# A row sum of squared differences: its 4 KB result stored by two queues instead of one

## The chip, the cores and the metric

The kernel runs on one core of a Trainium2 chip. The metric is the device time of one execution in microseconds, given as the median of several executions. The profile is taken from one more execution and lists what each engine and each DMA queue did and when. In it DVE is VectorE, ACT is ScalarE, POOL is GpSimd, SP is SyncE, and SPq is SP's own sequencer, which issues DMAs and waits for semaphores. PE, the matrix engine, has no work here.

## The reference

```
def setup_inputs():
    batch, dim = 1024, 4096
    return {
        "x": np.random.randn(batch, dim).astype(np.float32),
        "y": np.random.randn(batch, dim).astype(np.float32),
        "axis": -1,
    }

def reference(x, y, axis):
    return np.sum((x - y) ** 2, axis=axis).astype(np.float32)
```

Two float32 matrices of 16 MiB each are read, and 1024 float32 numbers, 4 KB, are written.

## The kernel before

Eight rows lie on each of the 128 partitions: partition p holds rows 8p to 8p+7, one after the other, as 32768 numbers. A transfer of some columns is thus one stretch per partition. The result has the same layout: `results` is a tile of 128 partitions by 8 numbers, and partition p's eight numbers, 32 B, go to one stretch of the output.

`X` and `Y` in the core's memory hold six of the eight rows each. Rows 6 and 7 go into the places of rows 0 and 1 once those have been squared. The loads are cut into the widths `xw` and `yw`: large ones first, small ones towards the end, so that little work is left when the last one has landed. All loads are issued by SP (`load`, L108), two of them ahead of the start-up barrier; those that go into used places wait for ACT (L221). Each load has a semaphore of its own.

DVE goes through the loads of `Y` in the order in which they are issued. For each it waits for the data, then subtracts in place (`sub`, L176) in pieces that don't cross a row. ACT squares each piece with an activation that sums along the row (`square`, L182); its sums go into `parts`, or into `results` where a row has one piece alone. DVE adds the parts of a row together (`complete`, L189). The last piece, 128 columns of row 3, is squared on DVE itself (L205) and adds the other part of its row; after it DVE completes row 7, the last sum of all. The order on each engine is the order of the program text: no scheduler moves anything. The engines are held together by the semaphores `diffs` (DVE to ACT), `acts` (ACT to DVE and SP) and `sums` (the sums that DVE has finished).

The end is this:

```
    nc.sync.wait_ge(sums, n["sums"])
    nc.sync.dma_start(out=ov, in_=results).then_inc(stored, 16)
    prog.close(nc.sync, stored, 16)
```

SP waits until all sums are there, issues one store of the whole of `results` (L233), and then goes into `close`. That clears the semaphores of the program in one range (L44) and waits until the store's completions have brought `stored` to 16 (L45), taking them away again. A DMA brings its semaphore up by 16 when all of it has landed. `stored` itself is not in the range that is cleared. Every semaphore made by `prog.semaphore` is, so that the next execution finds them at zero.

Of the kernel before, what the change touches and what calls it, by code (L numbers as in the profile page):

```python
# [47 lines left out]
def kernel(tc, x, y, axis, out):  # L48
    nc = tc.nc
    P = nc.NUM_PARTITIONS  # L50
# [11 lines left out]
    ov = out.rearrange("(p r) -> p r", p=P)  # L62
# [5 lines left out]
    results = nc.alloc_sbuf_tensor("results", [P, R], F32).ap()  # L68
# [22 lines left out]
    prog = Program(nc, tc)  # L91
    stored = nc.alloc_semaphore("stored")
    diffs = prog.semaphore("diffs")
    acts = prog.semaphore("acts")
    sums = prog.semaphore("sums")
    n = dict(diffs=0, acts=0, sums=0)

    def home(c0, c1):
        h0 = c0 % H
        return slice(h0, h0 + c1 - c0)  # L100
# [86 lines left out]
    def complete(r):  # L187
        nc.vector.wait_ge(acts, squared[row_parts[r][-1]])
        nc.vector.tensor_reduce(  # L189
            out=results[:, r : r + 1],  # L190
            in_=parts_of(r, len(row_parts[r])),
            axis=mybir.AxisListType.X,
            op=add,
        ).then_inc(sums, 1)
        n["sums"] += 1

    for j, (c0, c1) in enumerate(ys):
        final = j == len(ys) - 1
        wait_loaded(c1, landed_y[j][1])
        for piece in pieces_of(j, c0, c1):  # L200
            sub(*piece)
            r = piece[0] // D
            if final:
                nc.vector.wait_ge(diffs, n["diffs"])
                nc.vector.tensor_tensor_reduce(  # L205
                    out=Y[:, home(*piece)],
# [22 lines left out]
                complete(r)  # L229
    complete(7)  # L230

    nc.sync.wait_ge(sums, n["sums"])
    nc.sync.dma_start(out=ov, in_=results).then_inc(stored, 16)  # L233
    prog.close(nc.sync, stored, 16)


# [33 lines left out]
```

## Time and profile before

| what | value |
|---|---|
| median of 13 runs | 84.05 us (83.95 to 84.17) |
| the profiled execution's own time | 83.99 us |
| its span, first to last instruction | 82.7 us |
| DVE busy | 36.8 us (45%) |
| ACT busy | 33.4 us (40%) |
| DMA packets, bytes | 2736, 33.56 MB, mean 406 GB/s |
| share of 16 DMA engines in use | 95.9% |
| start of the store's issue on SP | 81.21 us |

The profiled execution took 83.99 us, of which the span accounts for 82.7; the rest lies before the first and behind the last instruction. All packets went over one hardware queue, SP's. Times inside the profile are counted from the start of the span. Waits and DMA issues of a sequencer are not counted as busy; the landing time of a DMA is counted from the start of its issue. The chain of waits is followed back from the last instruction that does work, at each step to what released it.

### The profile page before, as it was taken

The numbers are of one execution on the slowest core, as the hardware profiler recorded it, in microseconds if no ns is written. First come the engines' busy times: TensorE is split into PE (matmuls) and PEld (weight loads), VectorE is DVE, ScalarE is ACT, GpSimd is POOL, SyncE is SP. The second block draws the span as 40 slices with busy tenths as digits, with TensorE's granted clock in tenths as the row PEclk, the third lists the DMA queues.
The fourth block names the chain that finished last, engine by engine and source line by source line (L and its number), as shares of the span: only waits on it lengthen the run. The fifth ranks groups of instructions, "written<-read, shape, count | busy, mean of one in ns | idle before, by whom it ended". The sixth has DMA issues, their size and how long they took to land.

```text
span 82.7 us, 136 instructions
## 1 busy us (share of the span) xinstructions
DVE 36.8 (45%) x27; ACT 33.4 (40%) x41; POOL 0.2 (0%) x4
## 2 busy tenths in 40 slices
DVE  0000000000000000000299999999189996989982
ACT  0500000000000000000000979889896999899991
POOL 0000000000000000000000000000000000000000
DMA  6998998888999992899599899969989799999960
GB/s 135 396 484 381 618 523 381 381 381 381 504 503 503 503 503 126 378 503 503 254 507 507 349 412 507 476 285 507 413 350 508 344 442 440 420 407 410 398 213 2
DMA packets 2736, 33.56 MB, mean 406 GB/s; under 512 B 432, under 2 KB 1328, under 8 KB 1712
## 3 DMA queue, kind: packets, MB, share of 16 engines
q1 hardware_dynamic: 2736, 33.56, 95.9%
HBM read 33.55 MB, written 0.00 MB: 406 GB/s over the span
## 4 chain that ended last, share of the span: by engine, by line
DMA 63%; SPq 16%; DVE 12%; ACT 4%; issue 1%
DMA Y<-in_y_dram 63%; SPq L108 16%; DVE X L176 11%; ACT X L182 4%; DVE Y L205 0%; DVE results L189 0%; SPq L221 0%; DVE results L205 0%
## 5 line engine op out<-in xcount | busy, mean ns | idle before, releaser
L176 DVE TENSOR_TENSOR X<-X,Y 128x2048 f32<-128x2048 f32 (+10 forms) x21 | 36.2, 1779 | 44.4 <-DMA Y<-in_y_dram 44.1
L182 ACT ACTIVATE X<-X 128x2048 f32<-128x2048 f32 (+9 forms) x20 | 31.2, 1560 | 45.6 <-DVE X L176 45.6
L182 ACT ACTIVATION_READ_ACCUMULATOR X<-X 128x1 f32 x20 | 3.7, 186 | 0.0
L182 ACT ACT_TABLE_LOAD x1 | 1.3, 1283 | 1.9 <-PEq L19 1.9
L189 DVE TENSOR_REDUCE results<-parts 128x1 f32<-128x2 f32 (+2 forms) x4 | 0.4, 148 | 0.0
L205 DVE CUSTOM_DVE_ANT_0 Y<-X,parts 128x128 f32<-128x128 f32 x1 | 0.4, 351 | 0.0
L251 POOL MEMSET const-bfloat16-1.0<- 128x1 bf16 x1 | 0.1, 101 | 0.0
L251 POOL MEMSET const-uint8-127<- 128x1 uint8 x1 | 0.1, 101 | 0.0
L251 POOL MEMSET const-float32-0.0<- 128x1 f32 x1 | 0.1, 98 | 0.2 <-issue 0.2
L251 POOL MEMSET const-float32-1.0<- 128x1 f32 x1 | 0.1, 98 | 0.0
L205 DVE DVE_READ_ACCUMULATOR2_ANT results<- 128x1 f32 x1 | 0.1, 83 | 0.0
## 6 DMA issues: line engine op xcount, KB each, us to landing
Y<-in_y_dram SPq DMA_DIRECT2D x1, 8128.0 KB, 39.0
X<-in_x_dram SPq DMA_DIRECT2D x1, 6144.0 KB, 21.3
X<-in_x_dram SPq DMA_DIRECT2D x1, 4096.0 KB, 48.3
Y<-in_y_dram SPq DMA_DIRECT2D x1, 4096.0 KB, 57.5
X<-in_x_dram SPq DMA_DIRECT2D x1, 2736.0 KB, 13.3
X<-in_x_dram SPq DMA_DIRECT2D x1, 2048.0 KB, 7.2
Y<-in_y_dram SPq DMA_DIRECT2D x1, 1392.0 KB, 18.9
Y<-in_y_dram SPq DMA_DIRECT2D x1, 1312.0 KB, 16.1
```

The source lines that it names most:

```text
L108: nc.sync.dma_start(out=dst[:, home(c0, c1)], in_=src[:, c0:c1]).then_inc(sem, 16)
L176: nc.vector.tensor_sub(out=a, in0=a, in1=Y[:, home(c0, c1)]).then_inc(diffs, 1)
L182: nc.scalar.activation(out=a, in_=a, func=Square, accum_out=acc).then_inc(acts, 1)
L189: nc.vector.tensor_reduce(out=results[:, r : r + 1], in_=parts_of(r, len(row_parts[r])), axis=mybir.AxisListType.X, op=add,).then_inc(sums, 1)
L205: nc.vector.tensor_tensor_reduce(out=Y[:, home(*piece)], in0=X[:, home(*piece)], in1=X[:, home(*piece)], scale=1.0, scalar=parts_of(r, 1), ...
L251: nc = _bacc.Bacc("TRN2", target_bir_lowering=False, num_devices=1)
```

## The change

The store is cut into two halves by partitions. ACT waits for all sums and issues the store of the upper 64 partitions on its own queue; SP waits for the same and issues the store of the lower 64. Both count up `stored`, which now has to reach 32. Since `close` clears `sums` among others, SP must not begin it while ACT may still be waiting for `sums`; so ACT counts up a new semaphore `begun` behind its DMA, and SP waits for that before `close`.

```diff
@@ -93,6 +93,7 @@
     diffs = prog.semaphore("diffs")
     acts = prog.semaphore("acts")
     sums = prog.semaphore("sums")
+    begun = prog.semaphore("begun")
     n = dict(diffs=0, acts=0, sums=0)
@@ -229,9 +230,15 @@
                 complete(r)
     complete(7)
 
+
+    half = P // 2
+    nc.scalar.wait_ge(sums, n["sums"])
+    nc.scalar.dma_start(out=ov[half:P], in_=results[half:P]).then_inc(stored, 16)
+    nc.scalar.sem_inc(begun, 1)
     nc.sync.wait_ge(sums, n["sums"])
-    nc.sync.dma_start(out=ov, in_=results).then_inc(stored, 16)
-    prog.close(nc.sync, stored, 16)
+    nc.sync.dma_start(out=ov[0:half], in_=results[0:half]).then_inc(stored, 16)
+    nc.sync.wait_ge(begun, 1)
+    prog.close(nc.sync, stored, 32)
```

## The prediction, made before the changed kernel had run

> **What bounds the kernel now.** I read the timeline of the last microseconds first, because the diff touches only what follows the last sum; then SP's waits, the DMA view of the store alone, and last the chain of waits over the whole span.
>
> The end of the timeline (start, duration, engine, line, operation):
>
> ```profile
> 80.54 0.36 ACT L182 ACTIVATE X<-X 128x192 f32<-128x192 f32 x1
> 80.73 0.35 DVE L205 CUSTOM_DVE_ANT_0 Y<-X,parts 128x128 f32<-128x128 f32 x1
> 80.80 0.19 ACT L182 ACTIVATION_READ_ACCUMULATOR X<-X 128x1 f32 x1
> 81.01 0.08 DVE L205 DVE_READ_ACCUMULATOR2_ANT results<- 128x1 f32 x1
> 81.02 0.16 DVE L189 TENSOR_REDUCE results<-parts 128x1 f32<-128x8 f32 x1
> 81.21 0.34 SPq L233 DMA_DIRECT2D out_dram<-results  x1
> ```
>
> ACT is finished at 80.99 (80.80 + 0.19). The last sum ends at 81.18 (81.02 + 0.16), and SP begins the store 0.03 us later. From 81.21 to the end of the span at 82.7 nothing computes: this tail of about 1.45 us is the store alone, and all that the change can act on.
>
> SP's queue, waits from 78 us on (who waited for whom, total us, times, longest):
>
> ```profile
> SPq L233 <- DVE results L189: 8.1, 1, 8.1
> SPq L45 <- SPq L45: 1.0, 1, 1.0
> ```
>
> L45 is the last wait, in `close`, for the store's 16 completions. It stands open for 1.0 us: between issue and landing SP has only the range clear of the semaphores to do (L44, 68 ns, at 81.6).
>
> The DMA view from 82.0 to 82.5 (40 slices of 12.5 ns), and the store's line from the window 80 to 83:
>
> ```profile
> DMA  0000146853446343210000000000000000000000
> GB/s 0 0 0 3 13 28 41 44 24 19 26 28 29 23 19 16 11 5 5 0 0 0 0 0 0 0 0 0 0 0 0 0 0 0 0 0 0 0 0 0
> DMA packets 144, 0.00 MB, mean 8 GB/s; under 512 B 144, under 2 KB 144, under 8 KB 144
> ```
>
> ```profile
> out_dram<-results SPq DMA_DIRECT2D x1, 4.0 KB, 1.4
> ```
>
> The store is 128 rows of 32 B: 128 data packets and 16 completions, 144 in all, nine on each of 16 engines. They run from 82.04 to 82.23 (the first and the last slice that move anything). In the window 80 to 83 they take 2.6% of 16 engines' 3 us, so 0.026 x 3 x 16 / 144 = 8.7 ns each; one engine works 9 x 8.7 = 0.08 us. So the tail divides into four: **issue** 0.34 (81.21 to 81.55), **way to the engines** 0.49 (to 82.04), **packets** 0.19 (to 82.23), **receipt** about 0.4 (to 82.6, 1.4 us after the start of the issue). The engines are in use for 0.19 us of 1.4 and never more than eight tenths busy: the tail is latency, not bandwidth.
>
> The chain of waits, over the whole span, says that the rest is out of reach:
>
> ```profile
> DMA 63%; SPq 16%; DVE 12%; ACT 4%; issue 1%
> DMA Y<-in_y_dram 63%; SPq L108 16%; DVE X L176 11%; ACT X L182 4%; DVE Y L205 0%; DVE results L189 0%; SPq L221 0%; DVE results L205 0%
> ```
>
> The loads bind, and they are all issued before the first edited line. The chain ends at L189; the store's flight behind it appears in no share.
>
> **What the Trainium skill says.** "DMA: Bandwidth & Descriptors", section Rules for kernel authors, says of two transfers to disjoint partition halves not to bother: each half spreads over all 16 engines, from either queue, so they share them. The trace has one queue only, but agrees on the spread (144 packets, 16 completions). The section Anatomy of one DMA puts most of a small DMA's fixed time into the write receipt and the completion; here receipt and way, 0.4 and 0.49, are most of the 1.4. "Perfetto Trace Analysis", section DMA Instruction — HWDGE, says that an issue first waits for a lock on a descriptor generator which the issuing sequencers share, and that the recorded issue includes that wait. In this trace only SP issues, so two issues at once are not shown.
>
> **The change part by part.** The profiled execution took 83.99 us with its span of 82.7, so 1.29 lie around it; it is 0.06 below the median of 84.05. I work out what the tail gains or loses and add that to both.
>
> 1. *Everything before 81.18.* The instruction lists of the two kernels are the same on DVE and POOL, on SP up to the store, and on ACT up to a DMA row behind its last Activation. The loads, their waits and the order are untouched: 0. ACT's new wait for `sums` has no instruction of ACT queued behind it but the new DMA and the increment of `begun`, and nobody else waits for ACT's sequencer then. ACT's last row ends at 80.99, 0.19 before the sums are there, so ACT stands at its wait in time: 0.
>
> 2. *ACT picks up `sums`.* SP needed 0.03 (81.18 to 81.21). ACT's pauses behind DVE in the chain are 0.02 to 0.03. Both start at about 81.21: 0. Low end 0, high end 0.1 if a queue that has issued no DMA wakes more slowly.
>
> 3. *SP's half.* SP issues 64 rows instead of 128. Its issues last 0.33 to 0.34 after a wait (the load at 53.49, the store) and mostly 0.43 to 0.49 back to back, whether for 2624 or for 960 columns: the size of a row does not show. The number of rows is 128 in all of them, so half of it is not shown: between 0.17 (all scales) and 0.34 (none). I take 0.34, because the price did not follow the amount otherwise: 0.
>
> 4. *ACT's half.* One DMA issue on a queue that shows none before. Low end 0.17, as above; high end 0.68, if the generator is locked for the whole of SP's issue (0.34 + 0.34). I take 0.44, the usual price of an issue that follows directly on another: part of it behind SP's, most of it beside it. That is 0.10 after SP's: **+0.10**. It lies on the path, since the end waits for 32 completions and the later half sets them.
>
> 5. *Way, packets, receipt.* The way (0.49) and the receipt (0.4) begin anew for each half, side by side: 0. Data packets stay 128; completions go from 16 to 32, so each engine has 10 packets instead of nine: **+0.01**. Should each half's packets come out in half the time, up to 0.09 (half of 0.19) comes back; I take none of it, since both halves meet on the same engines.
>
> 6. *The wait for `begun`, the increment, one semaphore more in the clear.* Queued behind it on SP are the clear (68 ns) and the last wait. `begun` comes when ACT's issue ends, in my sum at 81.21 + 0.44 = 81.65, plus some 0.03; before, the clear stood at 81.6. The work that hides this is the store's own flight, the 1.0 us of L45. With that cover gone it would cost 0.1; to use it up, ACT's issue would have to end after 82.5, and then its half would land late anyway. 0.
>
> 7. *Around the span.* A second hardware queue may have to be made ready or put away, which no trace here shows. If the 1.29 around the span hold a share per queue, it is a fraction of them: low end 0, high end 0.3 as an estimate. I take 0.
>
> Sum: +0.10 + 0.01 = +0.11. On the profiled execution that is 84.10; on the median 84.05 + 0.11 = **84.16 us**. Changes of 0.2% (0.17 us) are about what a measurement of this kernel can tell from no change, and this lies within.
>
> **The rivals.**
> - *A, side by side (the forecast):* the later half lands 0 to 0.17 after the old store. 84.05 to 84.22, likeliest 84.16. For it: way and receipt carry most of the tail and overlap. Chance 0.48.
> - *B, slower, one lock:* the generator takes the halves one behind the other, and the second half starts its way when the first has left. At full price its issue lasts 0.68 and the landing goes back by 0.34: 84.05 + 0.34 + 0.01 = 84.40. It decides from the point where ACT's issue ends 0.16 later than SP's did, that is, beyond 0.50 us (0.34 + 0.16 + 0.01 for the packets is the bound of 0.17). For it: the lock that the skill describes, both queues released by one semaphore in the same instant, and 0.1 more for issues back to back. Against it: the packets' spread of 0.19 less 0.08 of work leaves only 0.11 in which the engines can have been fed one after the other, so the generator itself seems to need 0.1, not 0.34. A slower wake of ACT (part 2) and a cost per queue (part 7) fall on this side too. Chance 0.44.
> - *C, faster, half the rows in half the time:* both issues last 0.17 and the packets take 0.10: 84.05 - 0.17 - 0.09 = 83.79. For it: each queue does have half the rows. Against it: prices of issues that did not move from 2624 to 960 columns, and one set of engines. Chance 0.08.
> - *D, the change does not do what it says:* ACT could be held by its own work and issue late. Its 0.19 us of slack before the sums speaks against that, and the instruction list has the DMA on ACT; it would be a case of B. No chance of its own.
>
> **How the numbers follow.** The predicted time is A's, 84.16. The range takes all of A and B at its full price with 0.1 for a slow wake, 84.40 + 0.10 = 84.50, at the top; at the bottom 83.95, the lower measured bound of no change and a gain of 0.1 (the packets' 0.09). C's full gain, and B with more than its lock or a large cost per queue, are left out, about 2 in 10. A's own range is 84.05 to 84.22. The bounds of 0.2% fall at 83.88 and 84.22, so C is the chance of faster, A that of no change, B that of slower: 0.08, 0.48 and 0.44.
>
> **What the profile of the changed kernel would show.** Right: two DMA issues to `out_dram` at about 81.2, SP's of about 0.34, ACT's of about 0.44, 160 packets in the last microsecond, L45's wait still near 1.0, and a tail from the last sum of about 1.55 instead of 1.45. ACT's issue at 0.6 or more, or one issue starting where the other ends, shows B. Both near 0.17 to 0.25 show C. A tail that stays while the time around the span grows from 1.29 shows part 7. A last sum away from 81.2 would be the scatter of the loads, since nothing in the change reaches them. The forecast is wrong if the median goes beyond 84.22 or below 84.05 - 0.17 = 83.88.

## The result, and the profile after

The changed kernel takes 84.70 us in the median (84.58 to 84.94, 11 runs), the kernel before 84.08 beside it (48 runs). The ratio is 1.0074, with a 95% interval of 1.0065 to 1.0084: **slower by 0.62 us**, where the prediction had 0.11 and a range of 83.95 to 84.50.

The profiled execution took 85.02, of which 83.7 is span. It is 0.32 slower than the median, and the timeline of its end says why not to compare spans (start, duration, engine, line, operation):

```profile
81.28 0.19 ACT L183 ACTIVATION_READ_ACCUMULATOR X<-X 128x1 f32 x1
81.49 0.08 DVE L206 DVE_READ_ACCUMULATOR2_ANT results<- 128x1 f32 x1
81.50 0.16 DVE L190 TENSOR_REDUCE results<-parts 128x1 f32<-128x8 f32 x1
81.69 0.53 SPq L239 DMA_DIRECT2D out_dram<-results  x1
81.69 0.54 ACTq L236 DMA_DIRECT2D out_dram<-results  x1
```

The last sum ends at 81.66, 0.48 later than before: the loads were later in this one execution (SP's last two load issues began at 67.41, before at 67.02). The chain of waits still has their share first:

```profile
DMA 62%; SPq 16%; DVE 12%; ACT 4%; issue 1%
```

What counts is the distance from the last sum on. Both issues begin 0.03 behind it, as SP's did before. But they last **0.53 and 0.54** where SP's lasted 0.34, and they land late (the issues of the tail, us to landing in the last column):

```profile
out_dram<-results SPq DMA_DIRECT2D x1, 2.0 KB, 1.7
out_dram<-results ACTq DMA_DIRECT2D x1, 2.0 KB, 2.0
```

The old store landed 1.4 us after its start; the later half now takes 2.0. In the traces' own times the tail, from the end of the last sum to the end of the span, grows from 1.474 to 2.025 us. This 0.55 is nearly the whole loss of 0.62. The DMA view from 82.0 to 83.7 (40 slices of 42.5 ns) shows where the later half waits:

```profile
DMA  0000000000000000000031210012210000000000
GB/s 0 0 0 0 0 0 0 0 0 0 0 0 0 0 0 0 0 0 0 0 19 9 15 5 1 0 10 13 15 9 2 0 0 0 0 0 0 0 0 0
DMA packets 160, 0.00 MB, mean 2 GB/s; under 512 B 160, under 2 KB 160, under 8 KB 160
```

There are two separate stretches of packets, SP's from 82.85 and ACT's from 83.12, and a slice without any between them. The second half is not waiting for busy engines; its packets have not come to them yet.

SP's last wait, for all 32 completions, is the only one of SP's waits that grew, from 1.0 to 1.3:

```profile
SPq L45 <- SPq L45: 1.3, 1, 1.3
```

The clear of the semaphores stands at 82.3, behind `begun`, and is still hidden.

So there are two things to explain: a longer issue and landing for **each** half, and a second half that is another 0.3 behind the first.

### The profile page after: what moved, and what is told of

The parts are those of the page before. It is cut to its first block, busy times and chain, and to the rows that moved or that the text cites. A ratio compares the mean times of both kernels' runs of the same rounds, so it can differ in the third digit from the quotient of the medians.

```text
span 83.7 us, 138 instructions
## 1 busy us (share of the span) xinstructions
DVE 36.9 (44%) x27; ACT 33.5 (40%) x41; POOL 0.2 (0%) x4
## 4 chain that ended last, share of the span: by engine, by line
DMA 62%; SPq 16%; DVE 12%; ACT 4%; issue 1%
DMA Y<-in_y_dram 62%; SPq L109 16%; DVE X L177 11%; ACT X L183 4%; DVE Y L206 0%; DVE results L190 0%; SPq L222 0%; DVE results L206 0%
```

## The experiments

Three theories for the first four runs. **G**: two issues at once hinder each other at a descriptor generator that both sequencers share, as in the prediction's rival B. **R**: a store of 64 rows is itself slower than one of 128. **Q**: ACT's queue is slow. Times are medians; each ratio is to runs of the kernel before made beside that run, whose medians lie between 84.07 and 84.14. The cuts of code are against the changed kernel unless another is named, and `...` marks what is left out between the lines. A landing is counted from the start of the issue to the last completion; where two stores count up one semaphore, the profile gives the first 16 counts to the one that was issued first.

### SP's half alone

```diff
-    begun = prog.semaphore("begun")
...
-    nc.scalar.wait_ge(sums, n["sums"])
-    nc.scalar.dma_start(out=ov[half:P], in_=results[half:P]).then_inc(stored, 16)
-    nc.scalar.sem_inc(begun, 1)
...
-    nc.sync.wait_ge(begun, 1)
-    prog.close(nc.sync, stored, 32)
+    prog.close(nc.sync, stored, 16)
```

> Only SP's half is stored (the upper 64 partitions of the output are left unwritten); ACT has no store and no wait. Theory G (two issues at once hinder each other at a shared descriptor generator): SP's issue is back at about 0.34 us from 0.53, the landing at 1.4 or a little less from 1.7, and the time at 84.0 to 84.1. Rival R (a store of 64 rows is itself slower than one of 128): issue 0.53, landing 1.7, time about 84.35. Rival Q (ACT's queue is slow, above all at its first DMA): as G, since ACT is left out.

Measured: 84.32 beside 84.07, ratio 1.0028 (1.0014 to 1.0043). Timeline, and the issue with its landing:

```profile
81.27 0.53 SPq L235 DMA_DIRECT2D out_dram<-results  x1
```

```profile
out_dram<-results SPq DMA_DIRECT2D x1, 2.0 KB, 1.7
```

This is R: its issue and its landing, and a time 0.03 below its 84.35. With nothing beside it, SP's half has the same issue of 0.53 and the same landing of 1.7 as in the changed kernel. So ACT's issue costs SP's nothing that shows, and G is wrong about the longer issues. Storing **half** the result takes 0.25 longer than storing all of it (by the interval 0.12 to 0.36), and the tail of the profiled execution is 0.28 longer, 1.758 us.

### The whole store from ACT

```diff
-    half = P // 2
...
-    nc.scalar.dma_start(out=ov[half:P], in_=results[half:P]).then_inc(stored, 16)
+    nc.scalar.dma_start(out=ov, in_=results).then_inc(stored, 16)
...
-    nc.sync.wait_ge(sums, n["sums"])
-    nc.sync.dma_start(out=ov[0:half], in_=results[0:half]).then_inc(stored, 16)
...
-    prog.close(nc.sync, stored, 32)
+    prog.close(nc.sync, stored, 16)
```

> The whole store of 128 rows is issued by ACT alone; SP waits for begun and closes. G: ACT's issue about 0.34 to 0.38, landing 1.4, time 84.1, since nothing issues beside it. R: the same. Q: ACT's issue 0.54, landing 2.0 as in the changed kernel, time about 84.65.

Measured: 84.12 beside 84.07, ratio 1.0007 (0.9995 to 1.0019).

```profile
81.44 0.37 ACTq L235 DMA_DIRECT2D out_dram<-results  x1
```

The landing is 1.4. Q falls: ACT's queue does the old store in the old time, at its first DMA. Since this kernel also has the increment of `begun` and SP's wait for it, those cost nothing that shows either.

### Both halves from SP, one behind the other

```diff
-    begun = prog.semaphore("begun")
...
-    nc.scalar.wait_ge(sums, n["sums"])
-    nc.scalar.dma_start(out=ov[half:P], in_=results[half:P]).then_inc(stored, 16)
-    nc.scalar.sem_inc(begun, 1)
     nc.sync.wait_ge(sums, n["sums"])
+    nc.sync.dma_start(out=ov[half:P], in_=results[half:P]).then_inc(stored, 16)
     nc.sync.dma_start(out=ov[0:half], in_=results[0:half]).then_inc(stored, 16)
-    nc.sync.wait_ge(begun, 1)
```

> Both halves are stored by SP, one behind the other; ACT has no store. G: two issues of 0.34 and about 0.45 in a row, the second half lands about 0.4 later than the old store, time 84.45 to 84.5, thus earlier than with the two queues at once (84.70). R: two issues of 0.53 and landings of 1.7, time 84.9. Q: as G.

Measured: 85.27, ratio 1.0138 (1.0116 to 1.0159).

```profile
81.59 0.53 SPq L235 DMA_DIRECT2D out_dram<-results  x1
82.16 0.59 SPq L236 DMA_DIRECT2D out_dram<-results  x1
```

Two long issues in a row, as R says. The tail is 0.93 longer than before (2.402 us), near the 0.83 that R's 84.9 stands for; why the five runs lie another 0.3 higher is not shown. The last sum of the profiled one ended 0.38 later than before. The first of the two stores is the upper half: it is as slow as the lower.

### ACT's half behind SP's

```diff
+    go = prog.semaphore("go")
...
-    nc.scalar.wait_ge(sums, n["sums"])
-    nc.scalar.dma_start(out=ov[half:P], in_=results[half:P]).then_inc(stored, 16)
-    nc.scalar.sem_inc(begun, 1)
     nc.sync.wait_ge(sums, n["sums"])
     nc.sync.dma_start(out=ov[0:half], in_=results[0:half]).then_inc(stored, 16)
+    nc.sync.sem_inc(go, 1)
+    nc.scalar.wait_ge(go, 1)
+    nc.scalar.dma_start(out=ov[half:P], in_=results[half:P]).then_inc(stored, 16)
+    nc.scalar.sem_inc(begun, 1)
```

> The changed kernel with ACT's half held until SP has issued its own (SP counts up a semaphore go behind its DMA, ACT waits for it instead of for the sums). G: SP's issue 0.34 and landing 1.4; ACT's issue begins about 0.4 later, lasts about 0.34 to 0.4 and lands 1.4 to 1.5 after its start, so the end is at 84.5, no later than with both at once (84.70). R: SP 0.53, ACT 0.53 and 1.7 from a start 0.6 later, time about 85.0. Q: SP 0.34 and 1.4, ACT 0.54 and 2.0 from a start 0.4 later, time about 85.1.

Measured: 84.95, ratio 1.0107 (1.0085 to 1.0129); R said 85.0.

```profile
81.43 0.53 SPq L237 DMA_DIRECT2D out_dram<-results  x1
82.04 0.53 ACTq L240 DMA_DIRECT2D out_dram<-results  x1
```

```profile
out_dram<-results SPq DMA_DIRECT2D x1, 2.0 KB, 1.7
out_dram<-results ACTq DMA_DIRECT2D x1, 2.0 KB, 1.7
```

Started 0.61 apart, both land 1.7 after their own start. Started together, the second needs 2.0. So the 0.3 is a queueing of one half behind the other, and it is gone when they don't come together; but holding ACT back costs more (84.95 against 84.70) than it saves.

### Halves by columns

Every store again has 128 rows, of 16 B now.

```diff
-    half = P // 2
+    half = R // 2
...
-    nc.scalar.dma_start(out=ov[half:P], in_=results[half:P]).then_inc(stored, 16)
+    nc.scalar.dma_start(out=ov[:, half:R], in_=results[:, half:R]).then_inc(stored, 16)
...
-    nc.sync.dma_start(out=ov[0:half], in_=results[0:half]).then_inc(stored, 16)
+    nc.sync.dma_start(out=ov[:, 0:half], in_=results[:, 0:half]).then_inc(stored, 16)
```

> The store is halved by columns: ACT writes columns 4 to 7 of all 128 partitions, SP columns 0 to 3, 16 B a row; waits and begun as in the changed kernel. Theory S (a store of 128 partitions has a short issue, one of 64 a long one, and what is behind the issue takes two stores one after the other): both issues 0.34 to 0.40, one half lands after 1.4, the other 0.1 to 0.26 later, time 84.2 to 84.35, so better than the halves by partitions (84.70) by 0.3 or more. Rival N (any second store in the tail costs the same 0.37, and each half's longer issue comes from its being half the bytes): issues 0.53, time 84.7. Rival P (the cost goes with the number of packets, here 256 data packets instead of 128): landing later still, 84.9 or more.

Measured: 84.25 beside 84.13, ratio 1.0016 (1.0008 to 1.0023). Timeline, then the DMA view over the same window as the one of the changed kernel:

```profile
81.21 0.35 SPq L239 DMA_DIRECT2D out_dram<-results  x1
81.22 0.38 ACTq L236 DMA_DIRECT2D out_dram<-results  x1
```

```profile
DMA  0279851000000000000000000000000000000000
GB/s 0 9 19 31 22 13 5 0 0 0 0 0 0 0 0 0 0 0 0 0 0 0 0 0 0 0 0 0 0 0 0 0 0 0 0 0 0 0 0 0
DMA packets 288, 0.00 MB, mean 2 GB/s; under 512 B 288, under 2 KB 288, under 8 KB 288
```

```profile
out_dram<-results SPq DMA_DIRECT2D x1, 2.0 KB, 1.4
out_dram<-results ACTq DMA_DIRECT2D x1, 2.0 KB, 1.6
```

S's forecast holds, and N and P fall. The same bytes over the same two queues at the same instant, with more packets (288 against 160), have short issues and **one** joint stretch of packets, from 82.06 to 82.31. The landings are 1.4 and 1.6, and the loss is 0.12 instead of 0.62.

This is the case that the prediction had in mind, but that its sum of +0.11 fits is luck. ACT's issue ends 0.04 later than SP's did before, where the sum has 0.10. What takes longer is the arrival of the completions. The trace has the time of every count on `stored`: before, the 16 counts come from 1.27 to 1.44 us after the last sum, one about every 0.01 us; here the 32 come from 1.28 to 1.62 at the same pace and in one row, although the last packet ends only 0.06 later than before (1.13 against 1.07). The last count is 0.17 later, and so is the end of the span. No run here tries two semaphores, which would tell whether the one that both stores count up is the reason.

### SP's half one step later

```diff
+    go = prog.semaphore("go")
...
     nc.sync.wait_ge(sums, n["sums"])
+    nc.sync.sem_inc(go, 1)
     nc.sync.dma_start(out=ov[0:half], in_=results[0:half]).then_inc(stored, 16)
```

> The changed kernel with one more semaphore increment on SP between its wait and its store, so that ACT's issue begins first by some 0.04 us instead of last by 0.005. If what lies behind the issues takes the stores in the order of arrival: ACT's packets come first, about 1.17 after its issue, SP's some 0.2 to 0.26 behind them; time 84.7, as before. If ACT's queue is served last by its nature: SP's packets still come first, ACT's last; time 84.7 to 84.75.

Measured: 84.72, ratio 1.0074 (1.0054 to 1.0094).

```profile
81.26 0.55 ACTq L237 DMA_DIRECT2D out_dram<-results  x1
81.32 0.53 SPq L241 DMA_DIRECT2D out_dram<-results  x1
```

```profile
out_dram<-results ACTq DMA_DIRECT2D x1, 2.0 KB, 1.7
out_dram<-results SPq DMA_DIRECT2D x1, 2.0 KB, 1.9
```

The places are exchanged: ACT, now first by 0.06, lands after 1.7, and SP after 1.9. In the changed kernel SP's issue began first, by 0.005 us, and its packets came 0.27 before ACT's; here ACT's packets come 0.27 before SP's. In both orders the half that came first was served first, whatever its queue.

### Which numbers of rows are slow

The next kernels have SP's store alone, of other counts of rows. Their edit is the one of the first experiment with another range, for instance:

```diff
-    nc.sync.dma_start(out=ov[0:half], in_=results[0:half]).then_inc(stored, 16)
+    nc.sync.dma_start(out=ov[0:96], in_=results[0:96]).then_inc(stored, 16)
```

> SP alone stores 32 partitions (the other 96 of the output are left unwritten). Theory S, with 128 partitions as the special shape: issue 0.5 to 0.55, landing about 1.7, time 84.3, as with 64. Rival M (the fewer the partitions, the longer the issue): issue 0.6 to 0.7, time 84.4 or more. Rival F (64 is slow by itself, for where it lies): issue 0.34, time 84.05.

> SP alone stores 96 partitions (32 of the output are left unwritten). Theory S: issue 0.5 to 0.55, landing 1.7 or a little more, time 84.3. Rival M: between 128 and 64, issue about 0.43, time 84.2. Rival F: issue 0.34, time 84.05.

Three more counts and places, chosen after these two:

> SP alone stores the 64 partitions 32 to 95 (the rest is left unwritten). If the count of 64 is what is slow, wherever it lies: issue 0.53, landing 1.7, time 84.35. If it is a whole half of the partitions, 0 to 63 or 64 to 127: issue 0.35, landing 1.4, time 84.1.

> SP alone stores 48 partitions, three an engine (the rest is left unwritten). If only 64 of the counts is slow: issue 0.35, landing 1.4, time 84.05. If counts in the middle between 32 and 96 are slow: issue 0.45 to 0.53, time 84.2 to 84.35.

> SP alone stores 60 partitions (the rest is left unwritten), a count that divides into 15 parts of four but not into 16. If four rows an engine are slow: issue 0.53, landing 1.7, time 84.35. If 64 itself is slow: issue 0.35 to 0.4, landing 1.4, time 84.1.

The timelines' lines of the five, in this order:

```profile
81.47 0.36 SPq L234 DMA_DIRECT2D out_dram<-results  x1
```

```profile
81.27 0.35 SPq L234 DMA_DIRECT2D out_dram<-results  x1
```

```profile
81.85 0.59 SPq L234 DMA_DIRECT2D out_dram<-results  x1
```

```profile
81.28 0.36 SPq L234 DMA_DIRECT2D out_dram<-results  x1
```

```profile
81.37 0.42 SPq L234 DMA_DIRECT2D out_dram<-results  x1
```

Each ratio is to its own runs of the kernel before (84.07 for 0 to 63, 84.12 or 84.13 for the others):

| partitions stored by SP alone | issue, us | landing, us | median, us | ratio to the kernel before (95%) |
|---|---|---|---|---|
| 0 to 31 | 0.36 | 1.4 | 84.03 | 0.9988 (0.9979 to 0.9996) |
| 0 to 47 | 0.36 | 1.4 | 83.99 | 0.9980 (0.9969 to 0.9991) |
| 0 to 59 | 0.42 | 1.3 | 84.06 | 0.9989 (0.9978 to 1.0001) |
| 0 to 63 | 0.53 | 1.7 | 84.32 | 1.0028 (1.0014 to 1.0043) |
| 32 to 95 | 0.59 | 1.8 | 84.55 | 1.0054 (1.0032 to 1.0075) |
| 0 to 95 | 0.35 | 1.4 | 84.12 | 1.0002 (0.9991 to 1.0013) |
| 0 to 127 (the kernel before) | 0.34 | 1.4 | 84.08 | |

I had expected (as S) that 128 is the special count. It is not: 32, 48 and 96 rows are as quick as 128. **64 is**, and it is slow in all three places where it was put: 0 to 63, 32 to 95, and 64 to 127 as the first store of both halves from SP. (The 84.55 of 32 to 95 is 0.2 over what was expected. Its issue is 0.06 longer than that of 0 to 63; the rest is not taken apart.) The 60 rows bear on one more reason. The Trainium skill, "DMA: Bandwidth & Descriptors", section Why a DMA increments its semaphore by 16 and not by 1, says that a DMA runs on the largest number of engines up to 16 that divides its rows: for 60 that is 15 engines with four rows each, and the trace has 75 packets, 60 and 15 completions. So four rows an engine are not what is slow, and 16 engines are not either, since 32, 48, 96 and 128 rows have 16 completions too.

### 64 rows of half the length, and rows in two pieces

These cuts are against SP's half alone.

```diff
-    nc.sync.dma_start(out=ov[0:half], in_=results[0:half]).then_inc(stored, 16)
+    nc.sync.dma_start(out=ov[0:64, 0:4], in_=results[0:64, 0:4]).then_inc(stored, 16)
```

> SP alone stores columns 0 to 3 of 64 partitions (the rest of the output is left unwritten): 64 packets of 16 B, not next to each other in the output. If the count of 64 is slow (by partitions, or by four packets an engine): issue 0.53, landing 1.7, time 84.3. If it is that 64 rows of 32 B make one unbroken stretch of 2 KB: issue 0.35, landing 1.4, time 84.05.

Measured: 84.36 beside 84.14, ratio 1.0028 (1.0014 to 1.0042).

```profile
81.43 0.53 SPq L234 DMA_DIRECT2D out_dram<-results  x1
```

The landing is 1.7, as with whole rows: neither the bytes nor an unbroken stretch in the output matter, the count does.

```diff
+    ov3 = ov.rearrange("p (a b) -> p a b", a=2)
+    rv3 = results.rearrange("p (a b) -> p a b", a=2)
-    nc.sync.dma_start(out=ov[0:half], in_=results[0:half]).then_inc(stored, 16)
+    nc.sync.dma_start(out=ov3[0:64, :, 0:3], in_=rv3[0:64, :, 0:3]).then_inc(stored, 16)
```

and the same with 32 in the place of 64:

> SP alone stores columns 0 to 2 and 4 to 6 of 64 partitions (the rest is left unwritten): 64 partitions, but 128 packets of 12 B, eight an engine. If 64 partitions on the source's side are slow: issue 0.53, landing 1.7, time 84.3. If four packets an engine (64 rows as the store counts them) are slow: issue 0.35, landing 1.4, time 84.05.

> SP alone stores columns 0 to 2 and 4 to 6 of 32 partitions (the rest is left unwritten): 32 partitions, but 64 packets of 12 B, four an engine. If 64 partitions on the source's side are slow: issue 0.36, landing 1.4, time 84.05, as with 32 whole rows. If four packets an engine are slow: issue 0.53, landing 1.7, time 84.3.

Measured: 84.49 with an issue of 0.60, and 84.53 with one of 0.69, both landing after 1.8 (ratios of 1.0044 both). These two don't tell what they were made for: both were slow, with longer issues and landings than 64 plain rows. A store whose rows are in two pieces seems to have a price of its own, which no run here takes apart.

### The cut at another place

```diff
-    half = P // 2
+    half = 96
```

> The changed kernel with the cut between partitions 96 and 97 instead of 64 and 65: SP stores 96 partitions, ACT 32. Theory T (a store of 64 rows is slow, and two slow ones follow each other; stores of other counts are not): both issues 0.34 to 0.40, landings 1.4 and 1.4 to 1.6, time about 0.1 over the kernel before, 84.2. If any cut by partitions costs: issues over 0.5, time 84.5 to 84.7.

Measured: 84.27 beside 84.14, ratio 1.0021 (1.0008 to 1.0034).

```profile
81.25 0.36 SPq L239 DMA_DIRECT2D out_dram<-results  x1
81.25 0.40 ACTq L236 DMA_DIRECT2D out_dram<-results  x1
```

```profile
out_dram<-results SPq DMA_DIRECT2D x1, 3.0 KB, 1.4
out_dram<-results ACTq DMA_DIRECT2D x1, 1.0 KB, 1.6
```

This is the changed kernel with one number changed, and 0.43 of its loss is gone (84.70 to 84.27). In the two cuts that were run in which neither part has 64 rows, one by partitions and one by columns, a store in two costs 0.12 to 0.13. The completions show the same here as for the columns: 32 counts in one row, from 1.26 to 1.63 us after the last sum.

## Why the prediction was wrong

**The loss of 0.62 divides in two.** SP's half alone is 0.25 over the kernel before (84.32 against 84.07). The second half beside it adds the other 0.37, where a second store of another count of rows added 0.12 to 0.13. In the tails, 1.474 before, 1.758 with SP's half alone and 2.025 with both, the two are 0.28 and 0.27. In the prediction's terms: part 3 with its way to the engines was put at 0 and is 0.28, part 4 at 0.10 and is 0.02, part 5 for the later half at 0.01 and is 0.25.

- *Part 1 (nothing before the last sum)* held: the stores follow 0.03 behind it, and the time around the span is 1.32 (85.02 less 83.7) against 1.29, so *part 7 (a cost around the span)* was rightly nothing.
- *Part 2 (ACT picks up `sums`)* held: both issues stand at 81.69.
- *Part 3 (SP's half)* **is the step that failed first.** It gave 0.17 to 0.34 and took 0.34; 0.53 was measured. The bounds were both drawn from the thought that fewer rows can't cost more, and nothing in the trace of before said so: every DMA in it has 128 rows. Its range left room for a gain and none for a loss. The way to the engines, which part 5 carried over unchanged, was mis-sized with it: from the end of SP's issue to its first packet it is 0.64, not 0.49. So the issue of 64 rows has 0.18 more and its way 0.15 more.
- *Part 4 (ACT's half)* took 0.44 and its range to 0.68 held the 0.54. But that is luck: its reason, part of it behind SP's issue, is not what was measured. SP's issue is 0.53 alone too, and ACT's ends only 0.02 behind it.
- *Part 5 (way, packets, receipt side by side: 0)* **is the second step that failed.** ACT's packets begin 0.89 after the end of its issue (82.23 to 83.12), 0.27 behind SP's. For halves by columns the 0 was nearly right for the way, with one joint stretch of packets, but not for the receipt, where the 16 further completions made the last one come 0.17 later (0.06 of it from the packets), not the 0.01 of the sum. In the changed kernel the two rows of completions are apart, so there it is the way that counts.
- *Part 6 (the wait for `begun`)* held: with the whole store on ACT the handshake is there and the ratio is 1.0007.

Rival B had the right sign, and it was right that one half queues behind the other although two sequencers issue them. It put that into the issue, at 0.34; it lies behind the issue, at 0.27. The section of the Trainium skill that the prediction named, on the lock on a generator ("Perfetto Trace Analysis", DMA Instruction — HWDGE), says that the recorded issue includes the wait for the lock. No issue whose count of rows was also run without another store beside it grew by more than 0.02 for the other, so the lock, if it is what orders them, doesn't show in the records. That the packets of the later half reach idle engines late is shown, and that the first to come was first served in the two orders that were run; that a generator is the place is only argued.

The same skill's rule not to split a transfer into halves of partitions ("DMA: Bandwidth & Descriptors", Rules for kernel authors) is borne out as advice by all the cuts that were run: they cost 0.12 to 1.20 over the store in one. Its reason, that the halves run on the same engines, is not what costs for halves of 64 rows: the engines are idle between SP's packets and ACT's.

**Open:** why 64 rows are slow where 32, 48, 60, 96 and 128 are not. The place, rows of 32 B rather than 16 B, and four rows an engine are excluded. Loads of 64 rows, longer rows, and counts between 64 and 96 or between 60 and 64 were not tried. What makes the second of two such stores wait 0.27 is open too. No version here beats the kernel before with the whole output written; with the store in one, ACT's queue and SP's don't differ beyond the noise.

## What to carry to other kernels

The 4 KB store at the end of this kernel is latency: before cutting such a store, ask what a second one can shorten. Here even the best cut lost 0.12 us. When a cut changes the shape of a DMA, the price of the old shape bounds nothing: measure the new shape alone first, and try another cut before blaming the queue. When the loads scatter, compare two profiled executions by the distance from the last sum, not by the span.

## What the runs showed that I had not expected

- A store of 64 rows from one queue has an issue of 0.53 to 0.59 us and lands after 1.7 to 1.8; of 32, 48, 60, 96 and 128 rows it is 0.34 to 0.42 and 1.3 to 1.4.
- Two such stores issued together are served one after the other, 0.27 us apart, in the order in which they came; two stores of 128 rows issued together send their packets in one stretch, and their 32 completions take 0.34 us to come in where 16 took 0.17.
- ACT's queue issues its first store of 128 rows in 0.37 us, against 0.34 on SP's, with the same landing of 1.4.
